# Hybrid attention and recurrence layer: the recurrent branch's x projections in three pieces of tokens instead of four

## The chip, the cores and the metric

The kernel runs on one core of a Trainium2 chip. Its time is the device time of one execution in microseconds (us), the median of several runs. The engines are TensorE (PE), VectorE (DVE), ScalarE (ACT), GpSimd (POOL) and SyncE (SP); each takes its instructions in the order in which they stand in its queue.

## What is computed

One decoder layer of width 1024 on 1024 tokens, with 16 learned tokens put ahead of them (1040 in all), everything in float32:

```python
u = rmsnorm(h, g_pre_mix)
z = u @ w_in                                  # 1024 x 1792
q, k, v, xr, yr = jnp.split(z, split_at, -1)  # 512 | 128 | 128 | 512 | 512
attn = sliding_window_attention_with_sinks(q, k, v, attn_sinks)   # window 128
xr = causal_depthwise_conv(xr, conv_w, conv_b)                    # 4 taps
hr = rg_lru(xr, w_a, b_a, w_x, b_x, lam)      # gates, then a scan over time
rec = gelu(yr) * hr
h = h + rmsnorm(concat([attn, rec]) @ w_out, g_post_mix)
u = rmsnorm(h, g_pre_ffn)
h = h + rmsnorm(square(relu(u @ w_ff1)) @ w_ff2, g_post_ffn)
return h[:, 16:]
```

## The kernel before

Every matrix product is done in split precision. An operand is split into a high part and the remainder (`split`, lines 94 to 101: a copy on ACT at L96, a subtraction on DVE at L99), and `mm3` (lines 123 to 133) issues three matmuls into one accumulator: high by high (L125), high by low (L130), low by high (L131). So each block of 128 rows costs three matmuls, and in the profile a product is recognised by the three lines L125, L130 and L131.

The normalised, transposed input lies as eight blocks of 128 channels by 1040 tokens (`u`, line 229). `project` (lines 265 to 276) multiplies a weight chunk of 128 output channels with it, one piece of tokens after the other: for each piece it takes a bank of the pool `acc`, which has two, runs `mm3` over the eight blocks (24 matmuls), and hands the bank to a sink that empties it. `ALL` is the list of four pieces, 272, 256, 256 and 256 tokens; `REAL2` is two pieces of 512 without the learned tokens.

The first stage (up to about 66 us) makes k, v and the first half of q, piece by piece. Then come eight steps of attention, two pairs of heads by four quarters (lines 777 to 788): `scores` (matmuls at L628 and L632, the softmax on ACT at L82 and on DVE) and, one step late, `attend` (transposes at L678, products at L696). In each step one of ten fills is issued by `next_fill`, in this order: x chunk 0, q 2, x chunk 1, q 3, x chunks 2 and 3, then the y chunks 0 to 3 (the last two after the attention). A fill is the projection of 128 channels. Those in the attention loop are issued under `deferred(FILL_LAG)`, which gives them a later priority by 1000 places, so that the planner puts them where the attention leaves PE free. The order on each engine is laid out before the run, by a planner that works with priorities and times of its own; on the chip every engine takes its queue in that order.

`fill_x` (lines 739 to 744) projects one x chunk by `ALL`. Its sink (`new_x`, L490) copies each piece from the bank into the chunk's tile on ACT; then `conv` (lines 717 to 728, L719 and L724) runs four passes over the whole tile on DVE. `fill_q` and `fill_y` use `REAL2`, with sinks at L479 (DVE) and L476 (ACT), and at L751 (DVE).

After the attention, `gates` (lines 805 to 827) multiplies each convolved chunk by block-diagonal gate weights, two 64-row products side by side (L818), in three pieces of 348, 348 and 344 tokens, and applies the sigmoid on ACT. `gather`, `decay`, `recur` and `rec_out` (L832 to L857) make the recurrence on ACT and DVE, with a scan at L852. Meanwhile PE does y fills and the attention's share of the output projection (`out_mm`, blocks 0 to 3); the blocks 4 and 5 need the recurrence's first half. From there on, to the end, the span is filled with the output projection and the feed-forward part.

Of the kernel before, what the change touches and what calls it, by code (L numbers as in the profile page):

```python
# [37 lines left out]
def hybrid_layer(  # L38
# [19 lines left out]
    def slot(tag, shape, dt=F32):  # L58
        uid[0] += 1
        return slab.tile(shape, dt, tag=tag, name=f"{tag}{uid[0]}", bufs=bufs[tag])  # L60

    def pair(tag, shape):
        return slot(tag, shape, F32R), slot(tag, shape, F32R)

    def bank(tag, shape=(P, 512)):
        uid[0] += 1
        return ps.tile(list(shape), F32, tag=tag, name=f"ps_{tag}{uid[0]}")
# [13 lines left out]
    def lut(*args, **kwargs):  # L81
        ins = nc.scalar.activation(*args, **kwargs).ins  # L82
        if last_lut[0] is not None:
            tc.add_manual_dep(
                ins, last_lut[0],
                mybir.DependencyInfo(
                    mybir.DependencyClass.NoSync, mybir.DependencyReason.DATA
                ),
                reason="lut",
            )  # L90
        last_lut[0] = ins.name
        return ins

    def split(hi, lo, src, eng=None):
        if eng is None:
            nc.scalar.copy(hi, src)  # L96
        else:
            eng.tensor_copy(hi, src)
        low = nc.vector.tensor_tensor(lo, src, f32(hi), op=ALU.subtract).ins  # L99
        mark[0] = low.name  # L100
        return low
# [21 lines left out]
    def mm3(dst, lhs, rhs, start, stop, after=None):  # L123
        (lh, ll), (rh, rl) = lhs, rhs
        ins = nc.tensor.matmul(  # L125
            dst, lh, rh, start=start, stop=False, skip_group_check=True
        ).ins
        if after:
            behind(after, ins)
        nc.tensor.matmul(dst, lh, rl, start=False, stop=False, skip_group_check=True)  # L130
        last_mm[0] = nc.tensor.matmul(  # L131
            dst, ll, rh, start=False, stop=stop, skip_group_check=True
        ).ins.name
# [131 lines left out]
    def project(w, pieces, sink):  # L265
        wh, wl = w
        for t0, n in pieces:
            acc = bank("acc")
            for kc in range(KC):
                uh, ul = u[kc]  # L270
                mm3(
                    acc[:, :n], (wh[:, kc, :], wl[:, kc, :]),
                    (uh[:, t0 : t0 + n], ul[:, t0 : t0 + n]),
                    kc == 0, kc == KC - 1,
                )
            sink(acc[:, :n], t0, n)
# [10 lines left out]

    ALL = [(0, 272), (272, 256), (528, 256), (784, 256)]
    REAL2 = [(16, 512), (528, 512)]

# [175 lines left out]
    def new_q():  # L468

        q = pair("b", [P, T])  # L470

        def sink_q(acc, t0, n):
            c = slice(t0 - NMETA, t0 - NMETA + n)
            for h in range(2):
                r = HALF[h]
                nc.scalar.activation(q[h][r, c], acc[r], AF.Copy, scale=-(HD ** -0.5))  # L476
            for h in range(2):
                r, o = HALF[h], HALF[1 - h]
                nc.vector.scalar_tensor_tensor(  # L479
                    q[h][o, c], acc[r], -(HD ** -0.5), f32(q[h][r, c]),  # L480
                    op0=ALU.mult, op1=ALU.subtract,
                )

        return q, sink_q

    def new_x(tag="d"):
        xr = slot(tag, [P, TT])

        def sink_x(acc, t0, n):
            nc.scalar.copy(xr[:, t0 : t0 + n], acc)  # L490

        return xr, sink_x
# [224 lines left out]
    def conv(c, xr, tag="d"):  # L717
        y = slot(tag, [P, TT])
        nc.vector.tensor_scalar(  # L719
            y, xr, prm[:, c, 3:4], prm[:, c, 4:5], op0=ALU.mult, op1=ALU.add  # L720
        )
        for k in (2, 1, 0):
            s = 3 - k
            nc.vector.scalar_tensor_tensor(  # L724
                y[:, s:], xr[:, : TT - s], prm[:, c, k : k + 1], y[:, s:],
                op0=ALU.mult, op1=ALU.add,
            )
        xc[c] = y
# [3 lines left out]
    def fill_q(j):  # L732
        def run(w):
            q, sink = new_q()
            project(w, REAL2, sink)
            qs[j] = q
        return run

    def fill_x(c):
        def run(w):  # L740
            xr, sink = new_x()
            project(w, ALL, sink)
            conv(c, xr, "b" if c == 3 else "d")
        return run

    def fill_y(c):
        def run(w):
# [5 lines left out]

            project(w, REAL2, sink)
            ys[c] = y
# [49 lines left out]
    def gates(c):  # L805
        ch, cl = pair("b", [P, TT])
        split(ch, cl, xc[c])


        z = [slot("c", [P, TT]) for _ in range(2)]  # L810
        for t0, n in ((0, 348), (348, 348), (696, 344)):
            acc = []
            for s in range(2):
                flip[0] += 1
                acc.append(bank(("s", "pt", "o")[flip[0] % 3]))
            for k, (a, b) in enumerate(((0, ch), (0, cl), (1, ch))):
                for s in range(2):
                    nc.tensor.matmul(  # L818
                        acc[s][:, :n], gw[HALF[s], a, c, :], b[HALF[s], t0 : t0 + n],
                        start=k == 0, stop=k == 2, skip_group_check=True,  # L820
                    )
            for s in range(2):
                lut(
                    z[s][:, t0 : t0 + n], acc[s][:, :n], AF.Sigmoid,
                    bias=prm[:, c, 5 + s : 6 + s],
                )
        rg[c] = z
# [51 lines left out]
    for c in range(NLRU):  # L879
        gates(c)  # L880
        if c < 2:
            gather(c)
# [629 lines left out]
```

## Time and profile before

| | |
|---|---|
| median of 3 runs | 953.03 us (952.98 to 953.38) |
| profiled execution | 953.59 us |
| its span | 951.9 us |
| granted clock of TensorE, mean | 0.998 |
| PE busy, matmuls | 941.2 us, 4712 |
| DVE busy, instructions | 659.2 us, 849 |
| ACT busy, instructions | 508.2 us, 858 |
| stretch of the attention and its fills | about 66 to 194 us |
| stretch of the gates | about 194 to 211 us |

The profile is one execution; its span runs from the first to the last instruction, and the execution's own time holds 1.7 us more. "PE ... L125 MATMUL ps_acc<-a,ws 128x272" is a matmul of line 125 that writes a bank of the pool `acc` from tiles of the groups `a` (here the input blocks) and `ws` (weights), 272 columns wide. The records of successive matmuls overlap, so the distance between starts tells the pace. In square brackets stands how long the engine was idle before an instruction and what released it.

### The profile page before, as it was taken

The page shows a single profiled execution, that of the slowest core. Times are in us where ns is not written, and L with a number is a line of the kernel's source. Part 1 is how long each engine was busy: PE and PEld are TensorE (multiplying, and loading weights), DVE is VectorE, ACT ScalarE, POOL GpSimd, SP SyncE. Part 2 cuts the span into 40 slices and gives each one's busy share as a digit, 9 for nine tenths or more (in the row PEclk, how much of TensorE's full clock was granted, in tenths as well). Part 3 has the DMA queues.
Part 4 walks back from the last instruction along what each step waited for, and adds up shares of the span by engine and source line. Part 5 has one row for each costly group of instructions (what it writes and reads, how often), then busy time and mean ns, then how long its engine had stood idle before and what let it go on. Part 6 is the DMA issues. An engine that isn't in the chain of part 4 may idle for free.

```text
span 951.9 us, 12417 instructions
## 1 busy us (share of the span) xinstructions
PE 941.2 (99%) x4712; PEld 787.7 (83%) x4712; DVE 659.2 (69%) x849; ACT 508.2 (53%) x858; POOL 131.4 (14%) x205
## 2 busy tenths in 40 slices
PE   9999999999999999999999999999999999999996
PEld 8999999877888878888888888888888888888885
DVE  6667798879855887665644465476667676769883
ACT  8546766568644564443555575653533343445441
POOL 4104546410021100010000000000121000001201
PEclk9999999999999999999999999999999999999999
DMA  8220011104225468674432354334777765647934
GB/s 272 57 67 23 24 45 42 49 23 128 79 108 174 153 206 280 199 230 145 166 101 88 111 193 127 102 111 131 190 165 179 200 194 180 197 133 201 242 65 89
DMA packets 88199, 130.21 MB, mean 137 GB/s; under 512 B 13702, under 2 KB 52630, under 8 KB 88140
## 3 DMA queue, kind: packets, MB, share of 16 engines
q1 hardware_dynamic: 78972, 104.44, 34.3%
q0 software_dynamic: 8880, 24.19, 12.2%
q8 instruction: 37, 0.61, 0.3%
q10 hardware_dynamic: 288, 0.79, 0.2%
q14 instruction: 22, 0.18, 0.1%
HBM read 109.93 MB, written 18.87 MB: 135 GB/s over the span
## 4 chain that ended last, share of the span: by engine, by line
PE 86%; DVE 7%; ACT 3%; issue 2%; DMA 2%; SPq 0%; DVEq 0%; POOL 0%; ACTq 0%
PE ps_acc L125 10%; PE ps_acc L131 10%; PE ps_acc L130 10%; PE ps_s L131 6%; PE ps_s L125 6%; PE ps_s L130 6%; PE ps_pt L130 6%; PE ps_pt L131 6%; PE ps_pt L125 6%; PE ps_o L131 5%; PE ps_o L130 5%; PE ps_o L125 5%; ACT c L82 1%; PE ps_o L696 1%; PE ps_acc L282 1%
## 5 line engine op out<-in xcount | busy, mean ns | idle before, releaser
L99 DVE TENSOR_TENSOR ws<-raw,ws 128x1024 fp32r<-128x1024 f32 (+1 forms) x69 | 82.6, 1198 | 71.2 <-ACT ws L96 24.6
L96 ACT CAST ws<-raw 128x1024 fp32r<-128x1024 f32 (+1 forms) x68 | 69.7, 1025 | 90.9 <-PE ps_o L130 33.6
L125 PE MATMUL ps_acc<-a,ws 128*128 128x256 f32 (+2 forms) x272 | 88.5, 326 | 0.7 <-DVE b L479 0.4
L96 ACT CAST ws<-e 128x1024 fp32r<-128x1024 f32 x41 | 43.0, 1050 | 85.1 <-PE ps_o L130 37.6
L130 PE MATMUL ps_acc<-a,ws 128*128 128x256 f32 (+2 forms) x272 | 87.8, 323 | 0.0
L131 PE MATMUL ps_acc<-a,ws 128*128 128x256 f32 (+2 forms) x272 | 87.5, 322 | 0.0
L99 DVE TENSOR_TENSOR b<-b,b 128x1024 fp32r<-128x1024 f32 (+2 forms) x50 | 58.9, 1178 | 27.6 <-PE ps_o L130 22.4
L96 ACT CAST b<-b 128x1024 fp32r<-128x1024 f32 (+2 forms) x49 | 50.0, 1020 | 41.0 <-DVE b L997 35.5
L99 DVE TENSOR_TENSOR ws<-e,ws 128x1024 fp32r<-128x1024 f32 x41 | 50.1, 1223 | 30.7 <-ACT ws L96 17.3
L683 POOL TENSOR_SCALAR_AFFINE_SELECT c<-c 128x512 fp32r<-128x512 f32 x64 | 55.5, 883 | 68.9 <-ACT c L96 54.9
L125 PEld LDWEIGHTS ps_acc<-a,ws 128*128 128x128 f32 x272 | 51.3, 189 | 5.5 <-issue 0.9
L131 PEld LDWEIGHTS ps_acc<-a,ws 128*128 128x128 f32 x272 | 51.2, 188 | 4.0 <-issue 0.2
L130 PEld LDWEIGHTS ps_acc<-a,ws 128*128 128x128 f32 x272 | 51.1, 188 | 3.6 <-issue 0.2
L125 PE MATMUL ps_acc<-ws,b 128*128 128x512 f32 (+1 forms) x120 | 46.3, 387 | 0.0
L131 PE MATMUL ps_acc<-ws,b 128*128 128x512 f32 (+1 forms) x120 | 46.2, 385 | 0.0
L130 PE MATMUL ps_acc<-ws,b 128*128 128x512 f32 (+1 forms) x120 | 46.0, 384 | 0.0
L125 PE MATMUL ps_pt<-ws,b 128*128 128x512 f32 x112 | 44.2, 395 | 0.0
L131 PE MATMUL ps_pt<-ws,b 128*128 128x512 f32 x112 | 44.1, 394 | 0.0
L130 PE MATMUL ps_pt<-ws,b 128*128 128x512 f32 x112 | 44.0, 393 | 0.0
L125 PE MATMUL ps_s<-ws,b 128*128 128x512 f32 x110 | 43.4, 395 | 0.0
L130 PE MATMUL ps_s<-ws,b 128*128 128x512 f32 x110 | 43.4, 394 | 0.0
L131 PE MATMUL ps_s<-ws,b 128*128 128x512 f32 x110 | 43.2, 393 | 0.0
(415 smaller groups left out, 2660.6 us busy)
## 6 DMA issues: line engine op xcount, KB each, us to landing
raw<-in_w_ff_dram SPq DMA_DIRECT2D x59, 512.0 KB, 3.5
e<-in_w_ff_dram SPq DMA_DIRECT2D x43, 512.0 KB, 3.9
a<-in_w_ff_dram SPq DMA_DIRECT2D x12, 512.0 KB, 5.9
s_dram<-a POOLq DMA_DIRECT2D x12, 512.0 KB, 4.0
raw<-in_w_in_dram SPq DMA_DIRECT2D x9, 512.0 KB, 3.7
c<-in_x_dram SPq DMA_DIRECT2D x8, 512.0 KB, 4.9
d<-in_x_dram SPq DMA_DIRECT2D x8, 512.0 KB, 4.6
out_dram<-raw SPq DMA_DIRECT2D x8, 512.0 KB
```

The source lines that it names most:

```text
L82: ins = nc.scalar.activation(*args, **kwargs).ins
L96: nc.scalar.copy(hi, src)
L99: low = nc.vector.tensor_tensor(lo, src, f32(hi), op=ALU.subtract).ins
L125: ins = nc.tensor.matmul(dst, lh, rh, start=start, stop=False, skip_group_check=True).ins
L130: nc.tensor.matmul(dst, lh, rl, start=False, stop=False, skip_group_check=True)
L131: last_mm[0] = nc.tensor.matmul(dst, ll, rh, start=False, stop=stop, skip_group_check=True).ins.name
L282: last_mm[0] = nc.tensor.matmul(acc[:, :n], w[k // 2][:, kc, :], u[kc][k % 2][:, t0 : t0 + n], start=k == 0 and kc == 0, stop=k == last an ...
L683: nc.gpsimd.affine_select(out=p_[:, :, s], in_=f32(p_[:, :, 0]), pattern=[[0, 4], [g, P]], compare_op=op, fill=0.0, base=0, channel_multip ...
L696: nc.tensor.matmul(two[:, :, oc : oc + w], v, p_.rearrange("p (j i) s c -> p j (i s c)", j=2)[:, :, pc : pc + w], start=n == 0 and k == 0, ...
```

## The change

The four x chunks are projected in the three pieces that the gates use, 348, 348 and 344 tokens, instead of the four pieces of `ALL`. The list gets a name, `THIRDS`, and `gates` uses it too, with the same values as before. The number of columns in all is the same; for each x chunk there are 72 matmuls instead of 96, and three copies to the tile instead of four. k, v and q 0 and q 1 still use `ALL`.

```diff
     ALL = [(0, 272), (272, 256), (528, 256), (784, 256)]
     REAL2 = [(16, 512), (528, 512)]
+    THIRDS = [(0, 348), (348, 348), (696, 344)]
...
     def fill_x(c):
         def run(w):
             xr, sink = new_x()
-            project(w, ALL, sink)
+            project(w, THIRDS, sink)
             conv(c, xr, "b" if c == 3 else "d")
         return run
...
         z = [slot("c", [P, TT]) for _ in range(2)]
-        for t0, n in ((0, 348), (348, 348), (696, 344)):
+        for t0, n in THIRDS:
             acc = []
```

## The prediction

> **What bounds the kernel now.** I read the page's busy times and its chain first, then the windows of the stage that the change touches, then the order of TensorE's (PE's) instructions in it, record by record.
>
> ```profile
> PE 941.2 (99%) x4712; PEld 787.7 (83%) x4712; DVE 659.2 (69%) x849; ACT 508.2 (53%) x858; POOL 131.4 (14%) x205
> ...
> PE 86%; DVE 7%; ACT 3%; issue 2%; DMA 2%; SPq 0%; DVEq 0%; POOL 0%; ACTq 0%
> ```
>
> PE is busy for 99% of the span and holds 86% of the chain that ended last. A matmul's record overlaps the next one, so I take the pace from the distance between starts. Time is to be had from two things only: fewer or cheaper matmuls, and the few places where PE's starts stand apart.
>
> ```profile
> 100.00:135.00 35.00, 34.55 (x235) 31.66 (x234) 31.40 (x50) 23.41 (x66) 18.63 (x32) 1.00 0.12 36
> 135.00:170.00 35.00, 34.41 (x273) 33.28 (x273) 28.64 (x49) 24.59 (x85) 19.93 (x30) 1.00 0.13 41
> 170.00:194.00 24.00, 24.00 (x117) 19.89 (x116) 20.62 (x27) 12.48 (x24) 8.36 (x11) 1.00 0.17 45
> 194.00:211.00 17.00, 17.00 (x110) 12.52 (x109) 11.43 (x13) 11.08 (x23) 3.09 (x2) 1.00 0.07 17
> 211.00:234.00 23.00, 22.81 (x98) 18.12 (x98) 21.17 (x19) 18.98 (x22) 3.01 (x2) 1.00 0.38 102
> ```
>
> ```profile
> L490 ACT COPY d<-ps_acc x16: 359/377/396, 69.5 to 169.3; 128x256 f32<-128x256 f32 x12, 128x272 f32<-128x272 f32 x4
> ```
>
> The columns of the windows are the stretch, its length, then busy time of PE, weight loads, VectorE (DVE), ScalarE (ACT) and GpSimd, PE's granted clock, DMA share and GB/s. By the last row, the copies of the x projections, these run until 169 us as filler between the attention's matmuls; 194 to 211 holds the gates, 211 to 234 the rest of the recurrence. DVE (31.40 of 35 us) and ACT are full enough that a late copy there can hold PE up. The granted clock is 1.00 throughout.
>
> **The pace of a matmul.** In PE's timeline, the first piece of x chunk 0 and the start of its second, then a run of 512 columns:
>
> ```profile
> 66.14 0.29 PE L125 MATMUL ps_acc<-a,ws 128*128 128x272 f32 x1
> ...
> 69.12 0.28 PE L125 MATMUL ps_acc<-a,ws 128*128 128x256 f32 x1
> ...
> 71.72 0.29 PE L628 MATMUL ps_s<-ws,b 128*128 128x256 f32 x1
> ...
> 175.74 0.39 PE L125 MATMUL ps_acc<-a,ws 128*128 128x512 f32 x1
> ...
> 181.26 0.39 PE L696 MATMUL ps_o<-c,b 128*128 128x256 f32 x2
> ```
>
> Between the first two rows lie 24 starts (eight 128-row blocks, three products each): 2.98 us / 24 = 124.2 ns for 272 columns. To the third row are 22 starts of 256 columns: 2.60 / 22 = 118.2 ns. Between the last two are 24 starts of 512 columns: 5.52 / 24 = 230.0 ns. The line through 256 and 512 has 0.437 ns a column and about 6.4 ns that every matmul pays.
>
> A piece of 348 is not run with 128 rows before. The nearest rows either side give 118.2 + 92 x 0.437 = 158.4 ns, and 156.6 ns at 344. The gates run this width, two 64-row matmuls side by side:
>
> ```profile
> 194.31 0.42 PE L818 MATMUL ps_s<-b,e 64*128 64x348 f32 x1
> ...
> 200.79 0.39 PE L131 MATMUL ps_acc<-a,ws 128*128 128x512 f32 x1
> 201.11 0.43 PE L818 MATMUL ps_s<-b,e 64*128 64x348 f32 x1
> ...
> 201.38 0.33 PE L818 MATMUL ps_s<-b,e 64*128 64x348 f32 x1
> ...
> 202.48 0.32 PE L818 MATMUL ps_o<-b,e 64*128 64x344 f32 x1
> 202.50 0.32 PE L818 MATMUL ps_pt<-b,e 64*128 64x344 f32 x1
> 202.75 0.50 PE L125 MATMUL ps_acc<-a,ws 128*128 128x512 f32 x1
> ...
> 209.14 0.42 PE L818 MATMUL ps_s<-b,e 64*128 64x348 f32 x1
> ```
>
> From 201.38 to 202.48 are seven pairs, 157 ns each. Both rows agree closely.
>
> **The change part by part.** *Matmuls.* One chunk now takes 24 x (124.2 + 3 x 118.2) ns = 11.49 us. After, by the line, 24 x (158.4 + 158.4 + 156.6) = 11.36 us; by the gates' pace, 72 x 157 = 11.30 us. The tokens stay 1040, so only the fixed part of 24 matmuls and weight loads per chunk goes. Over four chunks that is 0.52 us by the line, 0.76 us by the gates; I take 0.52, since its rows have the same 128 rows. A loss here is excluded, since the width lies between two that are measured.
>
> The Trainium skill bears on this term: "TensorE: Matmul & The Clock Gate", section "Wait — 56ns, not 53.3ns?", says that back-to-back starts stand N / 2.4 GHz plus about 2.5 ns apart. By that the 96 matmuls fewer would save 0.24 us, not 0.52; the trace's 118.2 ns at 256 columns is above the 109.2 ns that the rule gives, and the trace decides.
>
> *Copies to the x tile on ACT.* From the groups by form in this stage:
>
> ```profile
> L96 ACT CAST c<-ps_pt 128x512 fp32r<-128x512 f32 x14 | 8.2, 584 | 1.1 <-PE ps_pt L678 1.0
> L490 ACT COPY d<-ps_acc 128x256 f32<-128x256 f32 x12 | 4.5, 376 | 2.1 <-PE ps_acc L131 2.1
> L490 ACT COPY d<-ps_acc 128x272 f32<-128x272 f32 x4 | 1.6, 391 | 0.0
> ```
>
> Four copies are 0.391 + 3 x 0.376 = 1.52 us a chunk; three at about 0.45 us (between 376 ns at 256 and 584 ns at 512) are 1.35. ACT is relieved of 0.17 us a chunk, 0.7 us in all. I count this at nothing: PE runs filler while ACT works, and it would cost at most the same 0.7 us if that cover were gone. The convolution on DVE reads the whole x tile and is unchanged; it starts after the last copy as before. Weight loads by DMA and their split are unchanged.
>
> *Waits for a bank.* The filler writes two banks in turn, so a piece waits for the copy of the piece but one before. Where PE's starts stand apart:
>
> ```profile
> 101.29 0.29 PE L131 MATMUL ps_acc<-a,ws 128*128 128x272 f32 x1
> 102.02 0.35 PE L125 MATMUL ps_acc<-a,ws 128*128 128x256 f32 x1 [0.44 <-DVE b L479]
> ...
> 157.43 0.60 PE L678 MATMUL ps_pt<-ident,c 128*128 128x128 f32 x4
> 158.33 0.39 PE L628 MATMUL ps_s<-b,b 128*128 128x256 f32 x1 [0.30 <-DVE c L646]
> ...
> 158.79 0.28 PE L632 MATMUL ps_s<-b,b 128*128 128x256 f32 x1
> 159.35 0.39 PE L125 MATMUL ps_acc<-a,ws 128*128 128x256 f32 x1 [0.29 <-ACT d L490]
> ...
> 232.63 0.40 PE L131 MATMUL ps_o<-a,b 128*128 128x512 f32 x1
> 233.21 0.50 PE L130 MATMUL ps_pt<-a,b 128*128 128x512 f32 x1 [0.19 <-DVE a L99]
> ```
>
> At 101.29 x chunk 1 has finished its first piece, and the second waits for DVE to empty the bank of the q projection before it: 0.73 us where 0.12 is the pace, a loss of 0.61. A first piece of 348 lasts 24 x (158.4 - 124.2) ns = 0.82 us longer, more than the wait, so with the order as it is this wait goes. At 158.79 a piece of x chunk 3 waits for ACT's copy: 0.56 - 0.12 = 0.44 us. Longer pieces give that copy more time too, but ACT reached it late behind the attention's work, so I count it between 0 and 0.44, and take 0, since what held ACT stays. The wait at 158.33 (about 0.47 us) is the attention's own and is not touched. What is late next on the bank is ACT's or DVE's copy of a later piece.
>
> *What then sets the end of the stage.* From the chain in order of time:
>
> ```profile
> 209.21 0.35 PE ps_s L818
> 210.42 2.30 ACT c L82 x5
> ...
> 229.72 2.32 DVE c L852
> 232.04 1.13 DVE a L99
> 233.21 0.50 PE ps_pt L130
> ```
>
> From the last gates ACT and DVE need 24.0 us until the output projection can go on at 233.21, and PE has filler for nearly all of it: at 232.63 it lacks work for 0.58 - 0.23 = 0.35 us. So both limits nearly coincide. A gain ahead of the gates moves both and passes through; a change of the order can lengthen the chain's end without making PE's work longer.
>
> The sum with the order kept is -0.52 - 0.61 = -1.13 us, between -0.3 (the wait returns at another bank) and -1.8 (the gates' pace and the wait at 159.35 too). Against the profiled execution's 953.59 us (span 951.9, 1.7 around it) that is 952.5; that run stands 0.56 us above the median, so by the median it is 953.03 - 1.13 = 951.9. About 0.2%, 1.9 us, is what a measurement of this kernel can tell from no change; this forecast is inside it.
>
> **The rivals.** The order on each engine is laid out before the run by a planner that adds up times of its own; pieces of other lengths and 25 instructions fewer a chunk (24 matmuls, a copy) can shift filler against attention. That decides more than the sum.
>
> *Waits vanish.* If the new order also loses the waits at 158.33, 159.35 and 233.21 (0.47, 0.44, 0.35), the sum is -2.4 us. The gates add a further term: entering one of their groups costs 0.32 us for 0.23 at 200.79 and 0.27 for 0.16 at 201.11, leaving it 0.25 for 0.16 at 202.50, 0.3 us in all, and filler breaks the gates into six groups, the first entered at 194.31 and the last at 209.14; two groups fewer save 0.6. Together -3.0, 950.0 us; the limit, with one group left, is -3.9. For it: PE is otherwise full, so every wait lost counts. Against it: nearly all must go together.
>
> *Filler ahead of the gates.* The x projections end earlier in the plan, so y filler can be placed in front of the gates instead of behind. PE's total is then unchanged, but the 24.0 us of ACT and DVE start later by 0.230 us for each matmul, with only filler that has been used up to cover them. It decides from 13 matmuls (3.0 us less the 1.13 gained = +1.9); 16 give +2.6, 955.6 us, and one whole piece of 24 gives 5.5 - 1.1 = +4.4. For it: the margin at 232.63 is nil already. Against it: a gate's input comes from the attention's engines, and those are relieved a little.
>
> *Late copies.* A piece now has three hand-overs instead of four, but each bank is held for 24 x 158.4 ns = 3.8 us instead of 2.8. If ACT's copies are queued behind attention work, PE, which takes its queue in order, stops with the attention's matmuls behind it. At 0.5 us each (the 0.44 and 0.61 above), five such waits give 2.5 - 0.5 = +2.0, 955.0 us.
>
> That the change does nothing is no rival: the widths and counts are fixed by it.
>
> **How the numbers follow.** Order kept or changed without effect: 0.38. Waits vanish: 0.28. Filler ahead: 0.24. Late copies: 0.10. So faster by over 0.2% 0.28, within it 0.38, slower 0.34. The likeliest gives 951.9 (its own range 951.2 to 952.7). The range for 8 in 10 reaches from 949.6, near the limit of vanishing waits, to 956.5, between 16 and 24 filler matmuls ahead.
>
> **What would show it.** In the profile after: 288 matmuls of the x projections instead of 384, starts 157 to 159 ns apart; 12 copies at L490 of about 450 ns; no wait of half a microsecond after x chunk 1's first piece; 96 PE instructions fewer, 4616. The gates should begin near 193.2 us and the output projection resume near 232. I am wrong if the stretch before the gates is longer than now, or if PE lacks work for over a microsecond ahead of the output projection, or if the time moves after 234 us, where I expect nothing.

## The result and the profile after

| | before | after |
|---|---|---|
| median | 953.03 us (952.61 to 953.38, 5 runs) | 957.29 us (955.77 to 957.48, 5 runs) |
| profiled execution | 953.59 us, span 951.9 us | 957.48 us, span 955.7 us |

The ratio is 1.0042 (95% interval 1.0031 to 1.0054): 4.3 us slower, 0.8 us above the top of the range, where 1.1 us faster was forecast. First the page of the kernel after: busy times, and the shares of the chain that ended last.

```profile
PE 944.5 (99%) x4616; PEld 789.1 (83%) x4616; DVE 657.1 (69%) x849; ACT 508.8 (53%) x854; POOL 135.5 (14%) x205
...
PE 90%; DVE 3%; ACT 2%; issue 1%; DMA 1%; SPq 1%; DVEq 0%; ACTq 0%
```

PE has 96 matmuls fewer and is busy 3.3 us longer. The next views say where. PE's waits between 60 and 300 us (us in total, times, longest), the whole list:

```profile
PE ps_pt L125 <- ACT b L96: 1.1, 1, 1.1
PE ps_pt L131 <- DVE b L99: 1.0, 1, 1.0
```

None is left in the stretch that was changed: the waits at 101, 158, 159 and 233 us of the kernel before are all gone. Two new ones stand behind it. PE's timeline after, in the output projection:

```profile
259.20 0.40 PE L131 MATMUL ps_pt<-a,b 128*128 128x512 f32 x1
260.73 0.49 PE L125 MATMUL ps_pt<-a,b 128*128 128x512 f32 x1 [1.13 <-ACT b L96]
261.06 0.39 PE L130 MATMUL ps_pt<-a,b 128*128 128x512 f32 x1
262.49 0.80 PE L131 MATMUL ps_pt<-a,b 128*128 128x512 f32 x1 [1.04 <-DVE b L99]
263.08 0.63 PE L125 MATMUL ps_pt<-a,b 128*128 128x512 f32 x1
...
265.22 0.63 PE L131 MATMUL ps_pt<-a,b 128*128 128x512 f32 x1
265.64 0.44 PE L125 MATMUL ps_o<-a,b 128*128 128x512 f32 x1
```

At a pace of 0.230 us the starts at 260.73 and 262.49 are 1.30 and 1.20 us late. Then from 263.08 to 265.22 are five starts in 2.14 us, 0.428 each: nearly half pace. The seven distances from 262.49 to 265.64 take 3.15 us instead of 1.61, 1.5 us more. The windows after show it as the granted clock (the column behind POOL's):

```profile
258.00:260.00 2.00, 1.60 (x7) 0.96 (x6) 2.00 (x5) 0.00 (x0) 0.00 (x0) 1.00 0.00 0
260.00:262.00 2.00, 0.72 (x2) 0.30 (x2) 2.00 (x5) 1.22 (x2) 0.00 (x0) 1.00 0.69 256
262.00:264.00 2.00, 1.51 (x4) 1.22 (x5) 1.03 (x2) 0.68 (x2) 0.00 (x0) 0.58 0.02 6
264.00:266.00 2.00, 2.00 (x7) 1.57 (x6) 0.00 (x0) 0.13 (x2) 0.00 (x0) 0.56 0.81 270
```

So the 4 us are about 2.5 us of waits and 1.5 us of slow clock. To see that nothing else counts, PE's instructions are laid side by side, those behind the change counted from the end, since there both kernels issue the same ones (us from the span's start, worked out from the two traces):

| | before | after |
|---|---|---|
| first attention matmul of the stretch | 65.58 | 65.65 |
| first gate matmul | 194.31 | 194.21 |
| last gate matmul | 210.53 | 213.56 |
| 3100 places before PE's last | 245.10 | 244.69 |
| 3000 places before PE's last | 268.19 | 271.90 |
| PE's last | 944.35 | 948.53 |

At 245 us the kernel after is 0.4 us ahead. Between these 100 matmuls it falls from 0.41 ahead to 3.71 behind, 4.1 us, and the last lies 4.18 behind. PE was ahead; what is late is the recurrence's second half. Its last steps on DVE, in the timeline of the kernel before:

```profile
244.76 2.39 DVE L850 SCALAR_TENSOR_TENSOR c<-b,c 128x1040 f32<-128x1040 f32 x2 [1.39 <-ACT c L82]
...
249.38 4.53 DVE L852 TENSOR_TENSOR_SCAN c<-b,b 128x1040 f32<-128x1040 f32 x2
...
255.02 1.28 DVE L857 TENSOR_TENSOR d<-d,c 128x512 f32<-128x512 f32 x2
...
256.83 0.68 DVE L99 TENSOR_TENSOR b<-d,b 128x512 fp32r<-128x512 f32 x1
...
258.03 0.68 DVE L99 TENSOR_TENSOR b<-d,b 128x512 fp32r<-128x512 f32 x1
```

and after (a line number is one higher):

```profile
246.75 1.24 DVE L851 SCALAR_TENSOR_TENSOR c<-b,c 128x1040 f32<-128x1040 f32 x1 [1.69 <-ACT c L82]
247.91 1.22 DVE L99 TENSOR_TENSOR a<-raw,a 128x1024 fp32r<-128x1024 f32 x1
...
254.72 1.28 DVE L858 TENSOR_TENSOR b<-b,c 128x512 f32<-128x512 f32 x2
255.92 2.31 DVE L853 TENSOR_TENSOR_SCAN c<-b,b 128x1040 f32<-128x1040 f32 x1
...
261.75 0.68 DVE L99 TENSOR_TENSOR b<-d,b 128x512 fp32r<-128x512 f32 x1
```

The half begins 2.0 us later (246.75 against 244.76); the last gate is 3.0 us later. Then an output weight's split (247.91) and two output products (254.72) now stand ahead of the last scan, 1.14 + 1.20 us by the distance between starts. So the last scan ends at 258.2 instead of 253.9.

What PE needs next is the remainder of the product's last block (block 7), a split "b<-d". Several splits of the same name follow each other, so the right one has to be found. In the kernel before it is not the first of those shown: the high copy that belongs to that one, on ACT, starts at 255.06, while DVE is still at the product of the last chunk (255.02 to 255.70), so it splits an older piece. The next high copy, at 256.10, waits for that product.

```profile
255.06 0.62 ACT L96 CAST b<-d 128x512 fp32r<-128x512 f32 x1
...
256.10 0.62 ACT L96 CAST b<-d 128x512 fp32r<-128x512 f32 x1
```

So the remainder was ready at 258.71 (258.03 + 0.68), and PE asked for it here:

```profile
260.31 0.40 PE L131 MATMUL ps_pt<-a,b 128*128 128x512 f32 x1
```

That was 1.6 us to spare. After, it is ready at 262.43 (261.75 + 0.68), 3.7 us later (one piece fewer stands between the scan and it, which gives back 0.6 us), and PE, 0.4 us ahead, asks earlier: 3.7 - 1.6 + 0.4 = 2.5 us, the two waits.

Why the last gate is late is seen in the order on PE and ACT. PE's timeline after, then ACT's:

```profile
194.73 0.39 PE L697 MATMUL ps_o<-c,b 128*128 128x256 f32 x1
...
196.59 1.09 PE L697 MATMUL ps_o<-c,b 128*128 128x256 f32 x5
```

```profile
198.61 0.58 ACT L706 COPY c<-ps_o 64x512 f32<-64x512 f32 x1
199.21 1.06 ACT L96 CAST b<-b 128x1040 fp32r<-128x1040 f32 x1
...
200.62 0.61 ACT L96 CAST b<-c 128x512 fp32r<-128x512 f32 x1
```

The attention's last six products now lie behind the first gate instead of ahead of it, and its last copy and two splits stand among the sigmoids. Counted in PE's order, 239 filler matmuls of 512 columns stand ahead of the last gate, 225 before: 14 x 0.230 = 3.2 us, and the last gate is 3.03 us later. That the two agree so well is partly chance. Two further terms, estimated from the distances between starts in the two traces, nearly cancel: ahead of the first gate about 2 us of short and long waits are gone, and from the first gate to the last about 2 us are added, since the gates now lie in nine groups instead of six, with the attention's products among them.

### The profile page after: what moved, and what is told of

It is laid out like the page before. It is cut to its first block, busy times and chain, and to the rows that moved or that the text cites. A ratio compares the mean times of both kernels' runs of the same rounds, so it can differ in the third digit from the quotient of the medians.

```text
span 955.7 us, 12224 instructions
## 1 busy us (share of the span) xinstructions
PE 944.5 (99%) x4616; PEld 789.1 (83%) x4616; DVE 657.1 (69%) x849; ACT 508.8 (53%) x854; POOL 135.5 (14%) x205
## 4 chain that ended last, share of the span: by engine, by line
PE 90%; DVE 3%; ACT 2%; issue 1%; DMA 1%; SPq 1%; DVEq 0%; ACTq 0%
PE ps_acc L125 11%; PE ps_acc L130 11%; PE ps_acc L131 11%; PE ps_pt L131 6%; PE ps_s L131 6%; PE ps_pt L125 6%; PE ps_s L125 6%; PE ps_pt L130 6%; PE ps_s L130 6%; PE ps_o L130 5%; PE ps_o L131 5%; PE ps_o L125 5%; PE ps_o L697 2%; DMA c<-in_x_dram 1%; PE ps_s L629 1%
## 5 line engine op out<-in xcount | busy, mean ns | idle before, releaser
L130 PE MATMUL ps_acc<-a,ws 128*128 128x512 f32 (+3 forms) x240 | 82.8, 345 | 0.0
L125 PE MATMUL ps_acc<-a,ws 128*128 128x512 f32 (+3 forms) x240 | 82.7, 345 | 0.0
L131 PE MATMUL ps_acc<-a,ws 128*128 128x512 f32 (+3 forms) x240 | 82.1, 342 | 0.0
L125 PEld LDWEIGHTS ps_acc<-a,ws 128*128 128x128 f32 x240 | 45.1, 188 | 4.3 <-issue 0.7
L131 PEld LDWEIGHTS ps_acc<-a,ws 128*128 128x128 f32 x240 | 45.2, 188 | 3.7 <-issue 0.2
L130 PEld LDWEIGHTS ps_acc<-a,ws 128*128 128x128 f32 x240 | 45.1, 188 | 3.6 <-issue 0.4
```

Of the source, the lines that this page charges most:

```text
L125: ins = nc.tensor.matmul(dst, lh, rh, start=start, stop=False, skip_group_check=True).ins
L131: last_mm[0] = nc.tensor.matmul(dst, ll, rh, start=False, stop=stop, skip_group_check=True).ins.name
```

## The experiments

The theory: the order that the planner lays out decides the time, not the pieces; with the order of before the three pieces give what was summed. The rival: the pieces themselves cost it, by banks held longer and copies that come late. (Where an expectation uses letters, A is the first of the two.) To part the two, each engine's instructions were recorded as the program issues them, and a written list put PE's, ACT's and DVE's between about 65 and 265 us in an order of my choice, by dependencies that carry no wait. POOL's and SP's were left alone. In the traces of these kernels all recorded instructions have the line of the recorder (L81 to L83), so they are told by their tiles.

**Three pieces in the order of before** (96 matmuls and 4 copies left out of it):

```diff
+ORDER = {"PE": ..., "ACT": ..., "DVE": ...}   # the order of before
...
-    nc = tc.nc
+    nc = Recorder(tc.nc)
...
+    nc.pin(tc)
```

> The three pieces, with the instructions of TensorE, ScalarE and VectorE from the first x projection to the output projection put in the order of the kernel before (each matmul and copy of an x chunk at the place where the kernel before has done as many tokens). Theory A: the loss is the new order alone, which makes the second half of the recurrence late for blocks 6 and 7 of the output projection. Then this kernel has no wait at 259 us, a granted clock of 1.00 there, and the sum of the prediction: 951.9 to 952.7 us. Theory B: the loss comes with the pieces themselves (the longer hold of a bank, or ScalarE's longer copies, delay the attention). Then it stays at 955 us or above, with the wait at the output projection.

Measured: 951.97 us (951.56 to 953.11, 11 runs) beside 952.64; ratio 0.9993 (0.9985 to 1.0002). The last gate is at 208.87, and PE's last matmul stands 877.69 us behind the first attention matmul, where it was 878.77 before: 1.08 us gained in one trace of each, 1.13 forecast. By the medians it is 0.67 us, and the interval reaches no change. Its waits between 60 and 300 us are all short, none at 260:

```profile
PE ps_acc L82 <- ACT d L82: 0.5, 1, 0.5
PE ps_s L82 <- DVE c L82: 0.4, 1, 0.4
PE ps_pt L82 <- DVE a L82: 0.2, 1, 0.2
```

The total is what the prediction summed, for a kernel that the change does not make; its terms are looked at below. Each beside the kernel before, the planner's order is 4.3 us slower and the old order 0.7 us faster, so the new order costs 4.9 us.

**Four pieces in the order of after:**

```diff
-            project(w, THIRDS, sink)
+            project(w, ALL, sink)
...
+ORDER = ...   # the order of after, four pieces in the place of three
```

> The kernel before, four pieces, with the instructions of the three engines in the order of the changed kernel (mapped in the same way). Theory A: it is slow though no piece was changed, 956 to 958.5 us, with PE waiting 2 to 3 us for the splits of blocks 6 and 7 near 260 us and a lower granted clock after it. Theory B: the order does little; 952.5 to 953.5 us and no such wait.

Measured: 959.16 us (958.95 to 960.71); ratio 1.0071 (1.0058 to 1.0083). The two waits near 260 us, 0.76 and 1.19 us by the starts, come with the order and without the pieces. But they are not the whole loss of 6.5 us, which is 0.7 us above the top of what was expected. Four pieces don't fit this order: three waits of its own for ACT's copy make 3.7 us by the starts. The lower clock that was expected did not come in the profiled execution (mean 0.998).

```profile
PE ps_acc L81 <- ACT d L81: 3.2, 3, 1.3
PE ps_pt L81 <- DVE b L81: 1.0, 1, 1.0
PE ps_pt L81 <- ACT b L81: 0.6, 1, 0.6
```

The first row is what "late copies" would have looked like; the kernel after has none of it.

**The order of after, but the recurrence's second half as before** (16 instructions of ACT and 19 of DVE; on DVE the split and the products go behind the scans):

```diff
-L851, L99 (weight), L852, L851, L853, L852, L858 x2, L853, ...
+L99 (weight), L851 x2, L852 x2, L853 x2, L858 x4, ...
```

> The changed kernel in its own order, but for 19 VectorE and 16 ScalarE instructions of the recurrence's second half (chunks 2 and 3: square root, products, scans, the outputs and their splits), which stand in the order of the kernel before. If the order inside the second half costs about 2 us (a weight split and two output products stand ahead of the last scan), the wait near 260 us falls from 2.9 us to under 1 us, the clock stays up, and the time is 953 to 954.5 us. If what counts is only that the gates end 3 us later, the wait stays above 2 us and the time above 956 us.

Measured: 954.54 us (954.34 to 957.37, 11 runs); 1.002 (1.0011 to 1.0029). 2.8 us come back, though two waits remain, 0.57 and 1.01 us by the starts (under 1 us in all was expected). By the traces 0.9 us of what comes back are shorter waits and 1.5 us the slow clock, which this execution does not have:

```profile
259.95 0.97 PE L83 MATMUL ps_pt<-a,b 128*128 128x512 f32 x3 [0.41 <-DVE b L83]
261.76 1.89 PE L83 MATMUL ps_pt<-a,b 128*128 128x512 f32 x7 [0.84 <-DVE b L83]
```

**The order of after, but the attention ended ahead of the gates:**

```diff
 PE:  L697 x6 (the last products) ahead of the first L819
 ACT: L706, L96, L96 (copy and splits) ahead of the first sigmoid
```

> The changed kernel in its own order, but the last six products of the attention stand on TensorE ahead of the first gate matmul, and the last attention copy, its split and the split of gate chunk 3 stand on ScalarE ahead of the first sigmoid (2.2 us of ScalarE work that the changed kernel has among the sigmoids). If these are what makes the gates late, the last gate matmul comes 1.5 to 2.5 us earlier and the wait near 260 us shrinks by as much, to about 1 us: 954 to 955.5 us. If the gates are late for another cause (the y filler between them), the last gate matmul stays within 0.7 us of 213.6 us and the time within 0.7 us of 957.3 us.

Measured: 954.92 us (954.59 to 956.21, 7 runs); 1.0028 (1.0018 to 1.0039). The time is in the expected range, the reason given for it is not what happened: counted from the first attention matmul the last gate is only 0.4 us earlier (1.5 to 2.5 was expected), since the 14 filler matmuls still stand ahead of it. The waits near 260 us are 0.77 and 1.19 us, 0.5 us less than in the kernel after, and a wait of 0.6 us for POOL is new at 194 us. The profiled execution, one of the faster (954.59 us), has no slow clock.

**Both of these:**

> The changed kernel with the two moves of the runs before together: attention's tail ahead of the first gate, and the recurrence's second half in the order of the kernel before. If the two delays add up along one chain, the wait near 260 us (2.9 us changed, about 1.6 with either move) is gone or under 0.4 us, with no drop of the clock, and the time is 952 to 953.2 us. If each move alone already took what there is to take, the wait stays at 1.2 us or more and the time at 954 us or above.

Measured: 953.54 us (952.89 to 954.15, 11 runs) beside 952.76; 1.0007 (0.9998 to 1.0016). The result lies between the two expectations. One wait of 1.0 us by the starts is left near 259, and the one for POOL at 194 us stays:

```profile
260.25 1.90 PE L83 MATMUL ps_pt<-a,b 128*128 128x512 f32 x7 [0.84 <-DVE b L83]
```

For the five kernels, worked out from the traces in us from the first attention matmul:

| | before | after | second half as before | attention first | both |
|---|---|---|---|---|---|
| last gate matmul | 144.95 | 147.91 | 147.91 | 147.51 | 147.53 |
| remainder of block 7 ready | 193.13 | 196.78 | 195.87 | 195.84 | 194.94 |
| PE's matmul that needs it | 194.73 | 196.84 | 195.93 | 195.90 | 194.99 |

In the four kernels in which PE waits for it, PE starts 0.05 or 0.06 us after that split ends. Each of the two moves brings it forward by 0.9 us, both by 1.8: they add up. With both it is still 1.8 us later than before, with 1.6 to spare and PE 0.7 us ahead, which is the wait of 1.0 that stays. It goes with a last gate that is 2.6 us late. The 14 filler matmuls ahead of that gate, which neither edit moves, are the likely cause; no run took them out alone without moving the waits elsewhere.

**One chunk in thirds, the planner free:** x chunk 0 alone, and x chunk 2 alone.

```diff
-            project(w, THIRDS, sink)
+            project(w, THIRDS if c == 0 else ALL, sink)   # the other: c == 2
```

> Only x chunk 0 in three pieces, the other three in four, order left to the planner. Its order has the attention's last products behind the first gate, as in the changed kernel, and 235 matmuls of 512-column filler ahead of the last gate (225 before, 239 changed). If the filler ahead of the gates sets the loss, 10 matmuls at 0.230 us make the last gate 2.3 us late and the time 954.5 to 957 us. If the loss grows with the number of chunks in three pieces, a quarter of it, 953.5 to 954 us.

> Only x chunk 2 in three pieces, order left to the planner, which puts the attention's tail and the 225 filler matmuls ahead of the last gate as in the kernel before. If the order decides, no loss: 952 to 953 us, and no wait near 260 us. If the loss grows with the number of chunks, 953.5 to 954 us.

Measured: chunk 0 alone 961.42 us (960.87 to 963.05); 1.0095 (1.008 to 1.0111). Chunk 2 alone 952.57 us (952.34 to 953.29); 0.9998 (0.9989 to 1.0007). One chunk loses twice what four lose, another nothing. Chunk 2 alone came out as expected; chunk 0 alone missed both ranges, by over 4 us. Chunk 2 leaves the counts of filler ahead of the last gate at 225, chunk 0 makes them 235 with ten groups of gates instead of six, and its last gate is at 216.95. That is 6.2 us later than before, counted from the first attention matmul, where 10 filler matmuls make 2.3: the count of filler alone does not give the loss. The two largest rows of its waits between 60 and 300 us:

```profile
PE ps_o L697 <- POOL c L684: 2.5, 2, 2.0
PE ps_pt L131 <- DVE b L99: 1.9, 2, 1.0
```

The second row is the wait of the kernel after. The first, most of it at 180 us, I read as the other end of the same thing, filler that was spent early and is missing under the attention; no run shows that. So the loss does not follow the number of chunks in three pieces; it goes with the order that the planner makes of them.

**The filler held back.** The kernel after with one dependency more, an order on PE without a wait: y chunk 1 is not begun before the attention's last product, either whole or its second piece only.

```diff
     attend(*prev)
+    behind(last_attend[0], pieces_begun[-2])   # the other: pieces_begun[-1]
```

> The changed kernel with one order added: the first matmul of y chunk 1's projection stands behind the last product of the attention; all else is left to the planner, which now puts 144 matmuls of 512-column filler ahead of the attention's last product (205 changed, 180 before), 225 ahead of the last gate (239, 225) and the gates into four groups (nine, six). If the filler ahead of the recurrence is the cause of the loss, the wait near 260 us is gone and the time is 950.5 to 952.5 us, under both kernels. If the attention now lacks filler, PE waits between 170 and 194 us for the softmax instead, and the time is 953.5 us or more.

> As hold2, but only the second piece of y chunk 1 is held back: 168 filler matmuls ahead of the attention's last product, 221 ahead of the last gate, which is 18 fewer than in the changed kernel (4.1 us at 0.230 us), while six attention products and their copies still stand behind the first gate (worth 2.4 us in the run that moved them). If the filler count ahead of the last gate decides, 951 to 953.5 us; if the copies among the sigmoids decide, above 954 us.

Measured: 961.41 us (960.87 to 962.01; 1.0094, 1.0078 to 1.0109) and 957.94 us (957.09 to 959.09; 1.0056, 1.0044 to 1.0069). Both missed their first expectation. For the whole chunk the other that was written down came true: PE now waits inside the attention. For the second piece alone the time fits the other expectation, but not by its cause: PE's only row of waits is for POOL, 3.0 us in all. A window of the one that holds the whole chunk, and the largest row of its waits:

```profile
170.00:194.00 24.00, 17.68 (x74) 13.84 (x74) 14.93 (x26) 12.40 (x33) 11.39 (x16) 0.86 0.14 45
```

```profile
PE ps_o L702 <- POOL c L689: 5.4, 4, 2.3
```

PE is busy 17.7 of 24 us, waiting for POOL's selections, and the clock falls to 0.86. I read this as too little filler for both places: spent ahead of the gates it delays the recurrence, held back it is missing under the attention. So these two runs don't tell what the filler ahead of the gates costs by itself.

**A version that beats both.** The first kernel of these, with three instructions moved further (the expectation speaks of four): ACT's copy of x chunk 0's first piece ahead of a step's exponentials, DVE's copy of masked scores ahead of a pass of the convolution, and a split of an output weight ahead of the scan.

> The three pieces in the order of the kernel before, with the three waits of TensorE that this order still has taken out by moving four instructions: ScalarE's copy of x chunk 0's first piece ahead of the softmax exponentials (wait of 0.65 us at 73.8), a masked copy of the scores on VectorE ahead of a convolution pass (0.64 us at 156.5), and a split of an output weight ahead of the scan (0.35 us at 231.0). If TensorE's own stream sets the time and each of these waits counts in full, 1.6 us less than with the order kept, 950.0 to 950.8 us, faster than both kernels. If ScalarE or VectorE merely moves the wait to the next instruction, 951.5 us or more.

Measured: 951.48 us (950.91 to 952.43, 11 runs) beside 952.76; 0.9987 (0.9978 to 0.9996), faster than both kernels. Only 0.5 of the 1.6 us expected beyond the first kernel came, which is nearer to the other expectation: the three waits above are gone, but one came in their place at 108 us (0.57 us by the starts), and one of 0.30 at 122, which the list below is too coarse to show:

```profile
PE ps_acc L82 <- ACT d L82: 0.4, 1, 0.4
```

## Why the prediction was wrong, step by step

**The matmuls' pace: the width right, the saving mis-sized.** From the timeline after, x chunk 0 from its first start to its fortieth:

```profile
66.20 0.33 PE L125 MATMUL ps_acc<-a,ws 128*128 128x348 f32 x1
...
72.42 0.32 PE L125 MATMUL ps_acc<-a,ws 128*128 128x348 f32 x1
```

39 distances in 6.215 us are 159.4 ns, where 158.4 was forecast. Only 1 ns, but the saving is a small difference of large numbers. As means over neighbouring starts of one width in the projections between 60 and 200 us, without the distances that hold a wait, the kernel before has 117.9 ns at 256 columns and 124.6 at 272, the kernel after 159.3 at 348 and 157.5 at 344. A chunk took 24 x (124.6 + 3 x 117.9) ns = 11.48 us, and takes 24 x (2 x 159.3 + 157.5) ns = 11.43 us. Four chunks save 0.20 us, not 0.52. The term that was mis-sized is the straight line from 256 to 512 columns: its 6.4 ns of fixed part aren't there at these widths; 0.20 us over 96 matmuls are 2.1 ns. The Trainium skill's rule, "TensorE: Matmul & The Clock Gate", section "Wait — 56ns, not 53.3ns?", was set aside in the prediction for its level at 256 columns. Its level is wrong here (109.2 ns against 117.9), but its 2.5 ns, and the 0.24 us that followed, are close to the 2.1 ns and 0.20 us of the traces.

The copies came out as estimated (0.45 us):

```profile
L491 ACT COPY d<-ps_acc 128x348 f32<-128x348 f32 x8 | 3.6, 455 | 5.2 <-DVE d L725 3.4 <-PE ps_acc L131 1.6
L491 ACT COPY d<-ps_acc 128x344 f32<-128x344 f32 x4 | 1.8, 448 | 1.7 <-PE ps_acc L131 1.7
```

**The waits for a bank: right for the one, not for their sum.** The wait at 101 us (0.61) is gone, in the order of before too, and so is the one at 159 (0.44), which was counted at nothing. But in the order of before a new one of 0.66 us for ACT's copy stands at 74 us, and the attention's own at 156 us is 0.17 longer. That is the lower end that the prediction gave, "the wait returns at another bank". By the traces 0.89 us are gained ahead of the first gate: 0.20 by the pace, 0.61 + 0.44 - 0.66 - 0.17 = 0.2 by these waits, the remainder in smaller ones. Another 0.2 us is gained behind the gates. That 1.08 came out for 1.13 is thus luck in good part: each of its two terms came out at less than half, and smaller gains that were not in the sum filled it up.

**The order: here it failed.** "Order kept or changed without effect" got 0.38 and was the forecast, though the text before it says that the order "decides more than the sum". What happened is the rival "filler ahead of the gates", chance 0.24. Its point of decision (13 matmuls) fits the 14 found; its price does not: by its own rule 14 give 3.2 - 1.1 = 2.1 us, 955.1 us, and 957.29 was measured. The condition of "waits vanish" came true as well, all four waits are gone, but the gain went into the gates, which lie in nine groups where that rival counted on fewer than six.

**"So both limits nearly coincide": the wrong place.** The wait at 233.21 was taken for the recurrence's deadline. It was for an output weight's split that stood behind a scan on DVE (its releaser is "DVE a", a weight's tile, not "DVE b", the recurrence's). After, the same weight's split ends at 235.75 and the matmul that needs it starts at 236.14, 2.9 us later than before, and PE does not wait for it: it has other products to do until then. The deadline lies 27 us on, where PE comes to the second half's blocks, with 1.6 us to spare before. That is why "after 234 us, where I expect nothing" was wrong, and with it the step "a gain ahead of the gates moves both and passes through".

**The rival's price: terms missing.** It let the chain start 3.2 us late, with no slack. Three things were not in it: the order of the second half and the attention's end behind the first gate, each 0.9 us on block 7's remainder (the table of the five kernels), and what a pause does to the clock (1.5 us). What is left for the filler is at most 1.8 us there, not 3.2. Against all this stood a slack of 1.6 us, at another place than the one that was found to have none.

**The range: short by the clock.** One of the five runs took 955.77 us with a mean granted clock of 0.998, the other four 956.61 to 957.48 with 0.996 or 0.997. Two thousandths of 955 us are 1.9 us, about the 1.5 measured between 262 and 266 us. I read the one run as free of the drop; it has no trace, so that is argued, not shown. It would lie inside the range. The kernel with the attention's end moved forward shows the same two groups: four executions of 954.59 to 954.92 us at 0.998 or 0.999, three of 956.09 to 956.21 us at 0.996 or 0.997. So a part of the 4.3 us comes and goes from one execution to the next.

**Open.** Why the planner shifts the order so for these lengths was not found. Waits and clock drop were not parted by a run of their own, and neither was the filler ahead of the gates from the rest of the order.

## What to carry to other kernels

When a planner lays out the queues, a change of a piece's length is a change of the order: cost both, and pin the old order to see the piece by itself. Find the deadline of a chain at each of its consumers, by the tile that the waiting instruction names, not at the nearest wait; where several pieces bear one name, find the one that the instruction needs. Filler that moves ahead of a chain's start is paid where that chain's last part is consumed, which may be tens of microseconds later, in code that nobody touched.

## What the runs showed of the hardware that was not expected

Two pauses of 1.30 and 1.20 us, 0.3 us of work between them, were followed by a granted clock of 0.58 and 0.56 over the next 4 us. The Trainium skill, "TensorE: Matmul & The Clock Gate", section "What's actually happening", has the clock go to half after an idle window of about 3.4 us that runs freely, whatever the kernel does. The half agrees with the 0.428 us a matmul here; no single pause was as long as 3.4 us, and that may be read as 2.5 idle us that fell into one window. Pauses alone did not settle it:

```profile
262.00:270.00 8.00, 5.81 (x23) 3.86 (x22) 6.50 (x12) 4.60 (x10) 0.00 (x0) 1.00 0.28 86
```

This window is of the kernel with chunk 0 alone: PE is idle 2.2 of 8 us, in three pauses, as long as in the kernel after from 258 to 264 us (0.40 + 1.28 + 0.49), and the clock is 1.00. That pauses of like length cost the clock in one execution and not in another fits a window that runs freely, and so do the two groups of times of one and the same kernel above; no run here was made to test it.
